# The start of a two-layer hybrid decoder: order of the first loads, and of ScalarE's first work

## The chip, the cores and the metric

The kernel runs on one core of a Trainium2 chip, in one launch. The metric is the device time of an execution in microseconds (us); lower is better. The engines are TensorE (PE in the profile; PEld are its weight loads), VectorE (DVE), ScalarE (ACT), GpSimd (POOL) and SyncE (SP), which only issues DMAs. ScalarE and GpSimd issue DMAs too.

## The reference

Two layers over 512 tokens of width 1024, in float32. Each layer normalizes x, projects it once, feeds four mixers (short convolution, sparse attention, gated recurrence, cross-attention into 256 memory tokens), sums them through gates, and ends with a SwiGLU feed-forward block. What matters here is the memory's path, which is computed before the layers, and the first norm of x:

```python
mem_n = rmsnorm(mem, mem_norm)
...
h = rmsnorm(x, norm_mix)                          # per layer; x @ w_in follows
...
mk, mv = jnp.split(mem_n @ mem_w_kv, 2, axis=-1)  # per layer, 1024 x 1024 weights
mk = rmsnorm(mk.reshape(b, MEM_TOKENS, MEM_HEADS, MEM_HEAD_DIM), mem_k_norm)
```

## The kernel before

**Products.** A float32 operand is written as a high and a low part in float32r, and a product is three matmuls (`mm3`, lines 260 to 262): high by high, high by low, low by high. So weights must be split before TensorE can use them. Class `Chunk` loads 1 MB of weights into a buffer `w_raw` (two of them, DMA issued by SyncE), and splits it in two parts of 128x1024: ScalarE copies to `w_hi` (line 97, through the helper `A`), and VectorE subtracts to `w_lo` (line 225). There are three buffers of each part.

**The order of the work.** The program is written as a list of operations. A compile-time scheduler sets the order on each engine from the order of the program, a priority (`tc.high_priority(offset=AHEAD)` puts the splits far ahead) and a simulated timeline. On the chip each engine and each DMA-issuing queue works through its list in order, so an operation that waits holds up all behind it on its engine. `tc.add_manual_dep(..., order, ...)` adds an order without a semaphore: it only says what comes first in that list.

**The start**, in the order of the program:

1. Constants, masks and 14 warm-up matmuls (`WARM`, line 144).
2. The memory is loaded whole into `mem_in` (line 150). Eight small loads bring the norms' gains and other parameters as 78 rows into the tile `rows` (line 157): those below row 40 from ScalarE's queue, the others from SyncE's. One transpose (line 160) turns them into columns, which ScalarE copies to `prm`. From there come the gains `g_mem`, `g_mix` and so on.
3. GpSimd's queue loads the four gains of the sparse attention's norms (lines 182 and 188, `gq_raw`, `gk`) and the positions (line 314); VectorE scales two of them (line 185).
4. `mem_in_T` transposes the memory, 8 columns of tiles by 2 (line 376). Each transposed column goes through one of the three `tr` buffers in PSUM; ScalarE writes `mt_hi`, multiplied by the gain, VectorE `mt_lo` (line 378). Then ScalarE squares and sums the memory for its norm (`mem_sq`).
5. `steps(mem_kv(0), first_h())` runs two generators in turn. `mem_kv` takes four chunks of the weights `mem_w_kv` of its layer, two for the keys and two for the values; each is 48 matmuls of 256 columns (8 tiles of the inner dimension, 2 of tokens, 3 by `mm3`). `first_h` loads x in two halves (line 391), squares it for its norm, transposes it (line 410) and writes the two parts of `h` (line 273), two columns of tiles at a step.
6. `rope_tables()` is VectorE's work. `mem_kv(1)` does the memory's keys and values for the second layer. Then the layers begin; their first product reads `h`.

Of the kernel before, what the change touches and what calls it, by code (L numbers as in the profile page):

```python
# [21 lines left out]
P = 128  # L22
S = 512
NT = S // P
D = 1024
# [44 lines left out]
def hybrid_trunk(ctx: ExitStack, tc: tile.TileContext, x, mem, positions, norm_mix, w_in, conv_w,  # L70
# [75 lines left out]
    n_rows = 78  # L146
# [3 lines left out]
    nc.sync.dma_start(mem_in, mem[0].rearrange("(t p) d -> p t d", p=P))  # L150
    for lo, src in ((0, norm_mix.rearrange("l (c p) -> (l c) p", p=P)),
                    (16, norm_ffn.rearrange("l (c p) -> (l c) p", p=P)),
                    (32, mem_norm.rearrange("(c p) -> c p", p=P)),
                    (40, conv_w.rearrange("l w (c p) -> (l w c) p", p=P)),
                    (64, hgrn_lower_bounds.rearrange("l (c p) -> (l c) p", p=P)),
                    (72, hgrn_out_norm), (74, mem_q_norm), (76, mem_k_norm)):
        (nc.scalar if lo < 40 else nc.sync).dma_start(rows[lo:lo + src.shape[0], :], src)
    prm = consts.tile([P, n_rows], F32, name="prm")
    ps = tr_ps()
    pe.transpose(ps[:, :n_rows], rows[:n_rows, :], ident[:n_rows, :n_rows])  # L160
    A(prm, ps[:, :n_rows], AF.Copy)
# [7 lines left out]
    def g_mem(c):  # L169
        return prm[:, 32 + c:33 + c]  # L170

    def g_conv(l, w, c):
        i = 40 + (l * 3 + w) * 4 + c
# [37 lines left out]

    class Chunk:
        def __init__(self, src, kt, n):
            self.kt, self.step = kt, min(kt, 1024 // n)
            raw = wpool.tile([P, 2048], F32, name="w_raw", bufs=RAW_BUFS)[:, :kt * n].rearrange("p (k n) -> p k n", n=n)
            nc.sync.dma_start(raw, src.rearrange("(k p) n -> p k n", p=P))
            self.parts = []
            for k in range(0, kt, self.step):
# [4 lines left out]
                with tc.high_priority(offset=AHEAD):  # L223
                    A(hi, raw[:, k:e], AF.Copy)
# [17 lines left out]
    def features(w, a, js, k0=0, kt=None, pss=None):  # L242
        """Feature-major products of the 128-column tiles js of a chunk."""
# [127 lines left out]

    def mem_in_T():
        for c in range(KD):
# [3 lines left out]
            A(mt[0][:, c, :], ps[:, :MEM], AF.Copy, scale=g_mem(c))  # L377
            dve.scalar_tensor_tensor(mt[1][:, c, :], ps[:, :MEM], g_mem(c), f(mt[0][:, c, :]),
                                     op0=OP.mult, op1=OP.subtract)
        for t in range(2):  # L380
            A(mem_sq, mem_in[:, t, :], AF.Square, scale=D ** -0.5, accum_out=mem_ss[:, t:t + 1])
# [6 lines left out]
    def first_h():  # L388
        xin = sp.tile([P, NT, D], F32, name="xin")
        for hf in range(2):  # L390
            nc.sync.dma_start(xin[:, 2 * hf:2 * hf + 2, :],
                              x[0, hf * 2 * P:(hf + 1) * 2 * P, :].rearrange("(t p) d -> p t d", p=P))
# [3 lines left out]
        for t in range(NT):  # L396
            A(mem_sq, xin[:, t, :], AF.Square, scale=D ** -0.5, accum_out=xs[:, t:t + 1])
# [19 lines left out]
    def mem_kv(l):  # L417
# [687 lines left out]
```

## Time and profile before

| | |
|---|---|
| timed runs | 2059.12 us median of 3 (2059.05 to 2059.2) |
| span of the profiled execution | 2057.1 us, 27077 instructions |
| timed runs less that span | 1.9 to 2.1 us, outside the first and last instruction |
| TensorE busy | 2046.8 us (99%) |
| VectorE, ScalarE, GpSimd busy | 1270.5, 1017.1, 9.8 us |
| granted TensorE clock, mean | 0.999 |
| DMA | 203.83 MB, mean 99 GB/s |

The span is that of one execution taken by the hardware profiler, from the first to the last instruction. The profile gives no time of that execution beside the span; the timed runs are other executions.

How to read its lines: a timeline has the start in us, the duration, engine, line of the kernel, operation, what is written `<-` what is read, shapes, and in brackets how long the engine had been idle and what ended that. A group's line has busy time, mean duration in ns and the idle time before it with its releaser. The chain of waits follows the work that ended last back through whatever released it. Matmuls overlap, so their durations are longer than the distance from one to the next.

### The profile page before, as it was taken

The page shows a single profiled execution, that of the slowest core. Times are in us where ns is not written, and L with a number is a line of the kernel's source. Part 1 is how long each engine was busy: PE and PEld are TensorE (multiplying, and loading weights), DVE is VectorE, ACT ScalarE, POOL GpSimd, SP SyncE. Part 2 cuts the span into 40 slices and gives each one's busy share as a digit, 9 for nine tenths or more (in the row PEclk, how much of TensorE's full clock was granted, in tenths as well). Part 3 has the DMA queues.
Part 4 walks back from the last instruction along what each step waited for, and adds up shares of the span by engine and source line. Part 5 has one row for each costly group of instructions (what it writes and reads, how often), then busy time and mean ns, then how long its engine had stood idle before and what let it go on. Part 6 is the DMA issues. An engine that isn't in the chain of part 4 may idle for free.

```text
span 2057.1 us, 27077 instructions
## 1 busy us (share of the span) xinstructions
PE 2046.8 (99%) x10588; PEld 1731.1 (84%) x10588; DVE 1270.5 (62%) x2513; ACT 1017.1 (49%) x1836; POOL 9.8 (0%) x33
## 2 busy tenths in 40 slices
PE   8999999999999999999999999999999999999999
PEld 8998988888888888888889898888888888888889
DVE  6779998547676544334457899953766754532542
ACT  7654655856665423223355456576657643322321
POOL 0000000000000000000000000000000000000000
PEclk9999999999999999999999999999999999999999
DMA  7632222212233232232242223321223332322322
GB/s 255 215 95 86 72 89 93 81 53 92 82 113 113 83 102 92 92 114 92 87 154 93 88 75 97 97 66 62 83 82 109 116 102 83 103 93 92 103 72 93
DMA packets 190783, 203.83 MB, mean 99 GB/s; under 512 B 4270, under 2 KB 182528, under 8 KB 190528
## 3 DMA queue, kind: packets, MB, share of 16 engines
q1 hardware_dynamic: 186944, 193.56, 29.2%
q10 hardware_dynamic: 3552, 8.41, 1.1%
q8 instruction: 83, 1.36, 0.3%
q14 instruction: 44, 0.36, 0.1%
q0 software_dynamic: 160, 0.13, 0.0%
HBM read 191.60 MB, written 10.49 MB: 98 GB/s over the span
## 4 chain that ended last, share of the span: by engine, by line
PE 98%; DMA 1%; DVE 0%; ACT 0%; SPq 0%; issue 0%; DVEq 0%; ACTq 0%
PE mm L261 30%; PE mm L260 30%; PE mm L262 30%; PE tr L705 1%; PE tr L699 1%; PE at L676 1%; PE at L675 1%; PE at L927 1%; DMA w_raw<-in_mem_w_kv_dram 1%; PE at L928 0%; PE at L260 0%; PE at L262 0%; PE at L261 0%; PE at L952 0%; PE tr L643 0%; PE tr L744 0%
## 5 line engine op out<-in xcount | busy, mean ns | idle before, releaser
L261 PE MATMUL mm<-h_lo,w_hi 128*128 128x512 f32 x1664 | 652.1, 392 | 0.0
L260 PE MATMUL mm<-h_hi,w_hi 128*128 128x512 f32 x1664 | 651.8, 392 | 0.0
L262 PE MATMUL mm<-h_hi,w_lo 128*128 128x512 f32 x1664 | 649.5, 391 | 0.0
L225 DVE TENSOR_TENSOR w_lo<-w_raw,w_hi 128x1024 fp32r<-128x1024 f32 (+1 forms) x348 | 419.7, 1207 | 350.7 <-ACT w_hi L97 349.5
L97 ACT ACTIVATE w_hi<-w_raw 128x1024 fp32r<-128x1024 f32 (+1 forms) x348 | 363.5, 1046 | 469.6 <-PE mm L261 416.8
L261 PEld LDWEIGHTS mm<-h_lo,w_hi 128*128 128x128 f32 x1664 | 312.6, 188 | 64.9 <-issue 2.5
L262 PEld LDWEIGHTS mm<-h_hi,w_lo 128*128 128x128 f32 x1664 | 312.4, 188 | 65.1 <-issue 1.4
L260 PEld LDWEIGHTS mm<-h_hi,w_hi 128*128 128x128 f32 x1664 | 312.6, 188 | 64.5 <-issue 2.0
L262 PE MATMUL mm<-w_hi,h_lo 128*128 128x256 f32 (+1 forms) x448 | 128.0, 286 | 0.0
L261 PE MATMUL mm<-w_lo,h_hi 128*128 128x256 f32 (+1 forms) x448 | 126.8, 284 | 0.0
L260 PE MATMUL mm<-w_hi,h_hi 128*128 128x256 f32 (+1 forms) x448 | 126.8, 285 | 0.0
L261 PE MATMUL mm<-a_lo,w_hi 128*128 128x512 f32 x272 | 106.1, 390 | 0.0
L260 PE MATMUL mm<-a_hi,w_hi 128*128 128x512 f32 x272 | 105.9, 389 | 0.0
L262 PE MATMUL mm<-a_hi,w_lo 128*128 128x512 f32 x272 | 105.6, 390 | 0.0
L260 PE MATMUL mm<-y_hi,w_hi 128*128 128x512 f32 x256 | 101.3, 397 | 0.0
L262 PE MATMUL mm<-y_hi,w_lo 128*128 128x512 f32 x256 | 100.2, 392 | 0.0
L261 PE MATMUL mm<-y_lo,w_hi 128*128 128x512 f32 x256 | 100.1, 391 | 0.0
L262 PEld LDWEIGHTS mm<-w_hi,h_lo 128*128 128x128 f32 x448 | 85.6, 191 | 1.4 <-issue 0.8
L260 PEld LDWEIGHTS mm<-w_hi,h_hi 128*128 128x128 f32 x448 | 85.2, 191 | 1.2 <-issue 0.8
L261 PEld LDWEIGHTS mm<-w_lo,h_hi 128*128 128x128 f32 x448 | 85.5, 191 | 0.6
L97 ACT ACTIVATE a_hi<-fg 128x512 fp32r<-128x512 f32 x44 | 27.8, 633 | 109.0 <-DVE fg L1054 109.0
L97 ACT ACTIVATE prob<-prob,small 128x128 f32<-128x128 f32 (+3 forms) x128 | 69.2, 555 | 15.2 <-DVE small L688 14.6
(351 smaller groups left out, 3048.6 us busy)
## 6 DMA issues: line engine op xcount, KB each, us to landing
w_raw<-in_w_in_dram SPq DMA_DIRECT2D x72, 1024.0 KB, 5.0
w_raw<-in_ffn_w_up_dram SPq DMA_DIRECT2D x44, 1024.0 KB, 5.1
w_raw<-in_w_lift_dram SPq DMA_DIRECT2D x32, 512.0 KB, 3.4
w_raw<-in_ffn_w_down_dram SPq DMA_DIRECT2D x16, 1024.0 KB, 5.0
w_raw<-in_mem_w_kv_dram SPq DMA_DIRECT2D x8, 1024.0 KB, 5.2
w_raw<-in_w_out_dram SPq DMA_DIRECT2D x8, 1024.0 KB, 4.9
kv<-kv ACTq DMA_DIRECT2D x8, 512.0 KB, 7.4
xT<-x_spill SPq DMA_DIRECT2D x16, 256.0 KB, 5.8
```

Of the source, the lines that this page charges most:

```text
L97: i = act.activation(dst, src, func, **kw)
L225: dve.tensor_sub(lo, raw[:, k:e], f(hi))
L260: pe.matmul(ps, ah, bh, start=first, stop=False)
L261: pe.matmul(ps, ah, bl, start=False, stop=False)
L262: pe.matmul(ps, al, bh, start=False, stop=last)
L675: pe.matmul(ps, q[:, hh, s], k[0][:, :n], start=True, stop=False)
L676: pe.matmul(ps, q[:, hh, s], k[1][:, :n], start=False, stop=True)
L699: pe.transpose(pp[:, (2 * e + i) * P:(2 * e + i + 1) * P], probs[2 * i + e][:, b * P:(b + 1) * P], ident)
L705: pe.matmul(pv[e * HD:(e + 1) * HD, :], vt[:, b, :], pt[:, b, e * 2 * P:(e + 1) * 2 * P], start=b == 0, stop=b == t)
L927: pe.matmul(pa[:, s], z[:, s], cmr[:, s], start=True, stop=True)
```

## The change

- The memory's gain is no longer among the 70 `rows` but is loaded as a tile of its own, `mem_row`, first on SyncE's queue, and transposed and copied to `mem_g` by itself. The transpose of `rows` and the copy to `prm` come after the memory's transposes in the program.
- The memory and the first weight chunk (`raw0`) are loaded in halves in turn: memory columns 0 to 511, weight rows 0 to 511, then the others. `Chunk` takes `raw0` instead of loading it.
- The small loads: convolution weights and recurrence bounds move from SyncE's queue to ScalarE's, the last three rows to GpSimd's.
- ScalarE's order: a chunk of layer 0's keys has its splits behind the memory copies that it needs (first part behind copy 4, second behind copy 8; the second chunk behind the last copy). The memory's squares come behind the last copy. x's squares come behind the last split that exists when `first_h` reaches them.
- `first_h` yields twice before it starts, so that the third chunk has been issued, and x's loads come behind it on SyncE's queue.

The diff without the renumbered rows and columns and a removed docstring:

```diff
@@ -143,22 +143,33 @@
     for _ in range(WARM):
         pe.matmul(ps[:, :P], ones_d, ones_d, start=True, stop=True)
     rows = sp.tile([P, P], F32, name="rows")
-    n_rows = 78
+    n_rows = 70
     warm = consts.tile([P, 1], F32, name="warm")
     A(warm, one, AF.Exp)
     mem_in = sp.tile([P, 2, D], F32, name="mem_in")
-    nc.sync.dma_start(mem_in, mem[0].rearrange("(t p) d -> p t d", p=P))
+    mem_row = sp.tile([KD, P], F32, name="mem_row")
+    nc.sync.dma_start(mem_row, mem_norm.rearrange("(c p) -> c p", p=P))
+
+    def w_raw(kt, n):
+        return wpool.tile([P, 2048], F32, name="w_raw", bufs=RAW_BUFS)[:, :kt * n].rearrange("p (k n) -> p k n", n=n)
+
+    raw0 = w_raw(KD, 256)
+    for hf in range(2):
+        cs = slice(hf * D // 2, (hf + 1) * D // 2)
+        nc.sync.dma_start(mem_in[:, :, cs], mem[0][:, cs].rearrange("(t p) d -> p t d", p=P))
+        nc.sync.dma_start(raw0[:, hf * KD // 2:(hf + 1) * KD // 2],
+                          mem_w_kv[0][cs, 0:256].rearrange("(k p) n -> p k n", p=P))
     for lo, src in ((0, norm_mix.rearrange("l (c p) -> (l c) p", p=P)),
                     (16, norm_ffn.rearrange("l (c p) -> (l c) p", p=P)),
-                    (32, mem_norm.rearrange("(c p) -> c p", p=P)),
-                    (40, conv_w.rearrange("l w (c p) -> (l w c) p", p=P)),
-                    (64, hgrn_lower_bounds.rearrange("l (c p) -> (l c) p", p=P)),
-                    (72, hgrn_out_norm), (74, mem_q_norm), (76, mem_k_norm)):
-        (nc.scalar if lo < 40 else nc.sync).dma_start(rows[lo:lo + src.shape[0], :], src)
+                    (32, conv_w.rearrange("l w (c p) -> (l w c) p", p=P)),
+                    (56, hgrn_lower_bounds.rearrange("l (c p) -> (l c) p", p=P)),
+                    (64, hgrn_out_norm), (66, mem_q_norm), (68, mem_k_norm)):
+        (nc.scalar if lo < 64 else nc.gpsimd).dma_start(rows[lo:lo + src.shape[0], :], src)
+    mem_g = sp.tile([P, KD], F32, name="mem_g")
+    ps = tr_ps()
+    pe.transpose(ps[:, :KD], mem_row, ident[:KD, :KD])
+    A(mem_g, ps[:, :KD], AF.Copy)
     prm = consts.tile([P, n_rows], F32, name="prm")
-    ps = tr_ps()
-    pe.transpose(ps[:, :n_rows], rows[:n_rows, :], ident[:n_rows, :n_rows])
-    A(prm, ps[:, :n_rows], AF.Copy)
 
     def g_mix(l, c):
         return prm[:, l * KD + c:l * KD + c + 1]
@@ -167,10 +178,10 @@
         return prm[:, 16 + l * KD + c:16 + l * KD + c + 1]
 
     def g_mem(c):
-        return prm[:, 32 + c:33 + c]
+        return mem_g[:, c:c + 1]
 
     def g_conv(l, w, c):
-        i = 40 + (l * 3 + w) * 4 + c
+        i = 32 + (l * 3 + w) * 4 + c
         return prm[:, i:i + 1]
 
     def col(i):
@@ -209,11 +220,14 @@
         dve.scalar_tensor_tensor(e, z, 0.0, e, op0=OP.min, op1=OP.subtract)
         A(dst, e, AF.Exp)
 
+    loads, splits = [], []
+
     class Chunk:
-        def __init__(self, src, kt, n):
+        def __init__(self, src, kt, n, raw=None, after=None):
             self.kt, self.step = kt, min(kt, 1024 // n)
-            raw = wpool.tile([P, 2048], F32, name="w_raw", bufs=RAW_BUFS)[:, :kt * n].rearrange("p (k n) -> p k n", n=n)
-            nc.sync.dma_start(raw, src.rearrange("(k p) n -> p k n", p=P))
+            if raw is None:
+                raw = w_raw(kt, n)
+                loads.append(nc.sync.dma_start(raw, src.rearrange("(k p) n -> p k n", p=P)))
             self.parts = []
             for k in range(0, kt, self.step):
                 e = min(kt, k + self.step)
@@ -221,7 +235,10 @@
                 hi, lo = (wpool.tile([P, 1024], F32R, name=nm, bufs=W_BUFS)[:, :m].rearrange("p (k n) -> p k n", n=n)
                           for nm in ("w_hi", "w_lo"))
                 with tc.high_priority(offset=AHEAD):
-                    A(hi, raw[:, k:e], AF.Copy)
+                    split = A(hi, raw[:, k:e], AF.Copy)
+                    splits.append(split)
+                    if after is not None:
+                        tc.add_manual_dep(split.ins, after[e - 1].ins.name, order, reason="after the copies")
                     dve.tensor_sub(lo, raw[:, k:e], f(hi))
                 self.parts.append((range(k, e), hi, lo))
 
...
@@ -369,16 +386,19 @@
     mt = (sp.tile([P, KD, MEM], F32R, name="mt_hi"), sp.tile([P, KD, MEM], F32R, name="mt_lo"))
     mem_r2, mem_r4 = small(4, name="mem_r2", bufs=1), small(4, name="mem_r4", bufs=1)
 
+    copies = []
+
     def mem_in_T():
         for c in range(KD):
             ps = tr_ps()
             for t in range(2):
                 pe.transpose(ps[:, t * P:(t + 1) * P], mem_in[:, t, c * P:(c + 1) * P], ident)
-            A(mt[0][:, c, :], ps[:, :MEM], AF.Copy, scale=g_mem(c))
+            copies.append(A(mt[0][:, c, :], ps[:, :MEM], AF.Copy, scale=g_mem(c)))
             dve.scalar_tensor_tensor(mt[1][:, c, :], ps[:, :MEM], g_mem(c), f(mt[0][:, c, :]),
                                      op0=OP.mult, op1=OP.subtract)
         for t in range(2):
-            A(mem_sq, mem_in[:, t, :], AF.Square, scale=D ** -0.5, accum_out=mem_ss[:, t:t + 1])
+            square = A(mem_sq, mem_in[:, t, :], AF.Square, scale=D ** -0.5, accum_out=mem_ss[:, t:t + 1])
+            tc.add_manual_dep(square.ins, copies[-1].ins.name, order, reason="after the copies")
         rstd_into(mem_r, mem_ss, small, 2)
         dve.tensor_copy(mem_r4.rearrange("p (a b) -> p a b", b=2), mem_r[:, :, None].to_broadcast([P, 2, 2]))
         dve.tensor_mul(mem_r2, mem_r4, mem_r4)
@@ -386,15 +406,20 @@
     norms = []
 
     def first_h():
+        yield
+        yield
         xin = sp.tile([P, NT, D], F32, name="xin")
+        last_load, last_split = loads[-1], splits[-1]
         for hf in range(2):
-            nc.sync.dma_start(xin[:, 2 * hf:2 * hf + 2, :],
-                              x[0, hf * 2 * P:(hf + 1) * 2 * P, :].rearrange("(t p) d -> p t d", p=P))
+            i = nc.sync.dma_start(xin[:, 2 * hf:2 * hf + 2, :],
+                                  x[0, hf * 2 * P:(hf + 1) * 2 * P, :].rearrange("(t p) d -> p t d", p=P))
+            tc.add_manual_dep(i.ins, last_load.ins.name, order, reason="after the weights")
         xs = small(NT, "xs", 1)
         r_t = small(NT, "rstd_t", 2)
         r_b = state.tile([P, S], F32, name="rstd", bufs=1)
         for t in range(NT):
-            A(mem_sq, xin[:, t, :], AF.Square, scale=D ** -0.5, accum_out=xs[:, t:t + 1])
+            square = A(mem_sq, xin[:, t, :], AF.Square, scale=D ** -0.5, accum_out=xs[:, t:t + 1])
+            tc.add_manual_dep(square.ins, last_split.ins.name, order, reason="after the weights")
         rstd_into(r_t, xs, small, NT)
         ps = tr_ps()
         for t in range(NT):
@@ -414,10 +439,11 @@
                 yield
         nc.scalar.dma_start(x_dram, xc)
 
-    def mem_kv(l):
+    def mem_kv(l, raw=None):
         kv = sp.tile([P, 4, 2, 2, MEM], F32R, name="kv", bufs=1)
         for q in range(2):
-            w = wchunk(mem_w_kv[l][:, q * 256:(q + 1) * 256], KD, 256)
+            w = Chunk(mem_w_kv[l][:, q * 256:(q + 1) * 256], KD, 256, raw if q == 0 else None,
+                      (copies if q == 0 else copies[-1:] * KD) if l == 0 else None)
             kus = []
             ms, r = small(4), small(4, "mk_r", 2)
             for t in range(2):
...
@@ -457,7 +483,10 @@
             nc.scalar.dma_start(kv_dram[l][:, 2 * q:2 * q + 2, 1], f(kv[:, 2 * q:2 * q + 2, 1]))
             yield
     mem_in_T()
-    steps(mem_kv(0), first_h())
+    ps = tr_ps()
+    pe.transpose(ps[:, :n_rows], rows[:n_rows, :], ident[:n_rows, :n_rows])
+    A(prm, ps[:, :n_rows], AF.Copy)
+    steps(mem_kv(0, raw0), first_h())
     rope_tables()
     steps(mem_kv(1))
     start.close()
...
```

More of the change, by code (lines that the diff above doesn't have):

```diff
@@ L443, in mem_kv @@
                 hi, lo = kv[:, 2 * q + j, 0, 0, :], kv[:, 2 * q + j, 0, 1, :]
-                A(hi, ps, AF.Copy, scale=col(76 + l))
-                dve.scalar_tensor_tensor(lo, ps, col(76 + l), f(hi), op0=OP.mult, op1=OP.subtract)
+                A(hi, ps, AF.Copy, scale=col(68 + l))
+                dve.scalar_tensor_tensor(lo, ps, col(68 + l), f(hi), op0=OP.mult, op1=OP.subtract)
             nc.scalar.dma_start(kv_dram[l][:, 2 * q:2 * q + 2, 0], f(kv[:, 2 * q:2 * q + 2, 0]))
@@ L468, in hybrid_trunk @@
     inv = consts.tile([P, H4], F32, name="inv")
-    a0, a1 = prm[:, 64:68], prm[:, 68:72]
+    a0, a1 = prm[:, 56:60], prm[:, 60:64]
     mx, e0, e1, sm, z0 = (small(H4, name=f"lb{i}", bufs=1) for i in range(5))
@@ L604, in mem_branch @@
                     with tc.high_priority(offset=AHEAD):
-                        A(qh, pq, AF.Copy, scale=col(74 + l))
+                        A(qh, pq, AF.Copy, scale=col(66 + l))
                         A(sq, pq, AF.Square)
-                        dve.scalar_tensor_tensor(ql, pq, col(74 + l), f(qh), op0=OP.mult, op1=OP.subtract)
+                        dve.scalar_tensor_tensor(ql, pq, col(66 + l), f(qh), op0=OP.mult, op1=OP.subtract)
                     pm = tr_ps()
```

2 lines of the change are left out of this document (1 added, 1 removed).

## The prediction

> **What bounds the kernel now.** I read the page first, then the chain of waits of the first 22 us, then the timelines of the engines there. From the page:
>
> ```profile
> span 2057.1 us, 27077 instructions
> PE 98%; DMA 1%; DVE 0%; ACT 0%; SPq 0%; issue 0%; DVEq 0%; ACTq 0%
> ```
>
> TensorE is the bound for 98% of the span. The edit touches only the start, so it can win only what TensorE loses before its stream of products becomes gapless. Three rows of TensorE's timeline show where that is:
>
> ```profile
> 1.12 5.04 PE L144 MATMUL tr<-ones_d 128*128 128x128 f32 x28 [1.12 <-DVE ones_d L118]
> 8.09 0.26 PE L160 MATMUL tr<-ident,rows 78*128 78x78 f32 x1 [1.94 <-DMA rows<-in_mem_k_norm_dram]
> ...
> 22.03 0.39 PE L261 MATMUL mm<-w_lo,mt_hi 128*128 128x256 f32 x1 [0.54 <-DVE w_lo L225]
> 22.25 0.28 PE L262 MATMUL mm<-w_hi,mt_lo 128*128 128x256 f32 x1
> 22.37 0.28 PE L260 MATMUL mm<-w_hi,mt_hi 128*128 128x256 f32 x1
> ```
>
> The warm-up ends at 6.16, the transpose of the parameter rows waits for a DMA until 8.09, and from 22.03 one 256-column product follows another every 0.12 us. The next window holds 46.47 busy us of 46.60, so nothing is lost behind 22.03:
>
> ```profile
> 22.00:68.60 46.60, 46.47 (x388) 46.12 (x389) 36.64 (x109) 36.13 (x91) 0.52 (x1) 1.00 0.75 255
> ```
>
> (TensorE, weight loads, VectorE, ScalarE and GpSimd busy, clock, DMA share, GB/s.) What TensorE did from 6 to 22 us, by groups:
>
> ```profile
> L260 PE MATMUL mm<-w_hi,mt_hi 128*128 128x256 f32 x17 | 5.4, 328 | 0.8 <-ACT w_hi L97 0.8
> L261 PE MATMUL mm<-w_lo,mt_hi 128*128 128x256 f32 x16 | 5.2, 333 | 0.8 <-DVE w_lo L225 0.8
> L262 PE MATMUL mm<-w_hi,mt_lo 128*128 128x256 f32 x16 | 5.2, 335 | 0.0
> L376 PE MATMUL tr<-ident,mem_in 128*128 128x128 f32 x16 | 3.1, 290 | 0.9 <-DVE mt_lo L378 0.9
> ```
>
> That is 49 products (the first chunk's 48 and one of the second) and 16 transposes. At 0.12 us each, with a transpose counted as a product (it has half the columns, so this is high), they need 65 x 0.12 = 7.8 us. They ended at 22.03, 15.9 us after the warm-up. Some 8.1 us is therefore all that can be won. The chain of waits says what took it:
>
> ```profile
> 0.81 5.40 DMA mem_in<-in_mem_dram
> 6.22 0.23 SPq L157
> ...
> 6.95 0.58 SPq L391
> ...
> 8.08 11.56 DMA w_raw<-in_mem_w_kv_dram
> 19.66 1.07 ACT w_hi L97
> 20.75 1.24 DVE w_lo L225
> ```
>
> The second weight chunk is issued behind x (L391), lands at 19.64, is split on ScalarE and VectorE, and only then TensorE runs free. The first chunk is issued after the wait of the sixth row load:
>
> ```profile
> SPq L157 <- DMA mem_in<-in_mem_dram: 3.5, 1, 3.5
> ```
>
> That load (6.22) is the ninth transfer of the SP and ScalarE queues together and waits for the first, the memory; that the ninth waits for the first is my reading.
>
> **The change, part by part.** Loads first. SP issues mem_row, half of the memory, half of chunk 0, the other halves, then chunk 1; x comes behind chunk 2.
>
> ```profile
> w_raw<-in_mem_w_kv_dram SPq DMA_DIRECT2D x8, 1024.0 KB, 5.2
> rows<-in_norm_mix_dram ACTq DMA_DIRECT2D x1, 8.0 KB, 3.2
> DMA packets 1539, 3.11 MB, mean 388 GB/s; under 512 B 42, under 2 KB 1027, under 8 KB 1539
> ```
>
> The last row is the window 8 to 16, with loads queued behind each other: 388 GB/s. The whole memory landed at 6.21; half of it is 0.52 MB less, 1.35 us, and its issue comes some 0.3 us later behind mem_row (0.23 for such an issue in the chain): 5.2. Each further half adds 1.35: chunk 0's first half 6.5, memory's second 7.9, chunk 0's second 9.2, and chunk 1 (2.7) at 11.9 instead of 19.64. The ninth transfer still waits for the first, but that is now a row of 4 KB (by the 8 KB row, 3.2 after issue, about 4.0), while the queue has bytes to move until 9. This costs nothing; if it hung on the first memory half (5.2) it still would not.
>
> One rule speaks against the halves. The Trainium skill, page "DMA: Bandwidth & Descriptors", section Bandwidth, advises batches of 1 MiB or more; by its fixed 2.0 us and 436 GB/s an isolated half would take 3.2 us, an estimate. The 388 GB/s of loads in a queue speaks for overlap; what a serial cost would do is rival 4.
>
> Now the engines. Their distances in the trace, from the rows' transpose at 8.09 on:
>
> ```profile
> 8.47 0.22 ACT L97 ACTIVATE prm<-tr 128x78 f32<-128x78 f32 x1
> 8.80 0.82 ACT L97 ACTIVATE mt_hi<-tr,prm 128x256 fp32r<-128x256 f32 x2
> 9.29 1.40 DVE L378 SCALAR_TENSOR_TENSOR mt_lo<-tr,prm,mt_hi 128x256 fp32r<-128x256 f32 x3
> 9.82 1.35 PE L376 MATMUL tr<-ident,mem_in 128*128 128x128 f32 x6 [0.65 <-DVE mt_lo L378]
> 11.51 2.00 ACT L97 ACTIVATE w_hi<-w_raw 128x1024 fp32r<-128x1024 f32 x2 [0.70 <-DMA w_raw<-in_mem_w_kv_dram]
> 12.59 1.23 DVE L225 TENSOR_TENSOR w_lo<-w_raw,w_hi 128x1024 fp32r<-128x1024 f32 x1 [0.85 <-ACT w_hi L97]
> 13.87 0.39 PE L261 MATMUL mm<-w_lo,mt_hi 128*128 128x256 f32 x1 [0.76 <-DVE w_lo L225]
> ```
>
> - The gain's transpose now needs mem_row alone (landed by 4) and starts when the warm-up ends: 6.17 instead of 8.09. Its copy (0.22) takes the place of prm's; the 70 rows' transpose goes behind the memory's work, where TensorE waits anyway.
> - First mt_hi 0.71 later, 6.88; first mt_lo 1.20 later, 7.37, done at 7.84 (0.47 each). The fourth column's transpose waits for that buffer (8.09 to 9.82 is 1.73): 7.90; its mt_hi about 0.5 later (less than the 0.71, which holds the gain's copy too), 8.4 to 8.8.
> - The order edge puts the first split behind that copy: w_hi 8.8 to 9.85 (its data landed at 6.5), w_lo 1.08 behind its start, 9.9 to 11.1, and the first full product 1.28 behind that: 11.2 instead of 13.87.
> - Second half: mt_lo of column 5 waits for w_lo, 11.1 to 11.6; the last column's transpose needs that buffer, its copy ends about 12.3. Second w_hi 12.3 to 13.3, w_lo 13.4 to 14.6, its products from 14.7. The first half's 24 products end at 11.2 + 2.9 = 14.1; the second half's 24 start at 14.7 and end at 17.6.
> - Chunk 1 (landed 11.9) is split on ScalarE 13.3 to 15.3 and on VectorE to 17.0; its first part is ready at 15.9, ahead of 17.6.
>
> So the gapless stream begins at 17.5 or so where it began at 22.03: 4.5 us won. The squares of the memory (two of 1.06 us that stood ahead of everything on ScalarE) move behind the copies; the norm they feed is first used behind chunk 0, and ScalarE has room there. Chunk 2 needs chunk 0's buffer (14.6) and 5.2 us to land, 19.8, split by 22.2; TensorE wants it at 17.5 + 48 x 0.12 = 23.3. Chunk 3 queues behind x: 19.8 + 8.1 (three chunks' bytes at 388 GB/s) is 27.9, split by 30.3, wanted at 29.1 and later by the key transposes. That is tight, about 1 us either way, and x's 32 transposes can fill it.
>
> The three small rows go to GpSimd's queue. Ahead of what?
>
> ```profile
> 1.34 0.71 POOL L182 DMA_DIRECT2D gq_raw<-in_dsa_q_norm_dram  x1 [0.34 <-issue]
> ...
> 2.92 0.57 POOL L182 DMA_DIRECT2D gq_raw<-in_dsa_q_norm_dram  x1
> ...
> 6.82 0.19 DVE L185 TENSOR_SCALAR gq<-gq_raw 128x64 f32<-128x64 f32 x1 [5.17 <-DMA gq_raw<-in_dsa_q_norm_dram]
> 7.52 0.20 DVE L185 TENSOR_SCALAR gq<-gq_raw 128x64 f32<-128x64 f32 x1 [0.50 <-DMA gq_raw<-in_dsa_q_norm_dram]
> ```
>
> Three issues of 0.57 to 0.71 us push both gq loads (and positions, and the masks' selects) back by 1.7 to 2.1 us. The gq multiplies wait for them on VectorE, and whatever the compiler queued behind them waits too: rival 1. Two more row loads on ScalarE's queue delay only the warm-up activation, which nobody waits for.
>
> Sum: the profiled span is 2057.1 and the timed runs lie at 2059.05 to 2059.2, so 2.0 us lie outside it and stay. Span 2052.6, time 2059.1 - 4.5 = **2054.6**. A measurement can tell about 0.2% from no change, here 4.1 us, so the forecast is just beyond it. If TensorE gets hi-hi products during its waits, more comes, up to the 8.1 bound: 2051.0.
>
> **Rivals.**
>
> 1. VectorE stands behind the gq loads. They now land at 8.5 and 9.2 to 9.6, and my first mt_lo is at 7.37. If both stand ahead of it, it starts at 9.5, everything slides by 2.0, and 2.5 are won: 2056.6. For it: both were ahead of every mt_lo before (6.82 and 7.52 against 9.29). Against: the compiler's order goes by readiness, and mt_lo is earlier now.
>
> 2. The clock drops again. For these three us it stood at 0.50:
>
> ```profile
> 15.00:18.00 3.00, 3.00 (x16) 3.00 (x16) 2.19 (x12) 2.97 (x7) 0.00 (x0) 0.50 1.06 366
> ```
>
> Half of 3 us is 1.5 lost: 3.0 won, 2056.1. Before, part of that loss lay under the wait for chunk 1; now nothing would hide it. Against: by 14.8 TensorE would have done some 24 products, where it had done 11 (2 and then one every 0.12 us from 13.87). The Trainium skill, page "TensorE: Matmul & The Clock Gate", Part 1, says that about 3.4 us without work halve the clock and 3.4 us of work restore it; by that rule the edit's shorter waits would keep it whole, and the trace agrees that sparse work preceded the drop.
>
> 3. ScalarE becomes the bound, and it is slower. From 22.0 to 68.6 it worked 36.1 of 46.6 us, 78%. x's squares move behind the third chunk's splits:
>
> ```profile
> 14.49 1.06 ACT L97 ACTIVATE mem_sq<-xin 128x1024 f32<-128x1024 f32 x1
> ...
> 15.67 1.06 ACT L97 ACTIVATE mem_sq<-xin 128x1024 f32<-128x1024 f32 x1
> ...
> 57.69 0.74 DVE L273 SCALAR_TENSOR_TENSOR h_lo<-xc,prm,h_hi 128x512 fp32r<-128x512 f32 x1
> ...
> 68.67 0.40 PE L260 MATMUL mm<-h_hi,w_hi 128*128 128x512 f32 x1
> ```
>
> From one square to the next it is 1.18. That puts 4 x 1.18 = 4.7 us of squares, and 2.4 of the memory's, into that stretch: 43.2 us. At 78% it takes 55.4 us from 17.5, so h's first product comes at 72.9 instead of 68.67: 4.2 us slower, 2063.3. It decides once ScalarE cannot be used above 43.2 / (64.2 - 17.5) = 93%. Against: much of its idle time was waiting for TensorE, which now comes earlier, and h had 10 us to spare.
>
> 4. The halves pay their fixed part in series, so the edit does not do what it says: 5.2 less 2.7 for the bytes is 2.5 us per load, two loads more are 5.0, and the 4.5 are gone: 2059.1.
>
> **How the numbers follow.** The forecast, 2054.6, has 0.42, more than the 4.5 won through hi-hi products 0.12; rival 1 has 0.18, rival 2 0.11, rival 4 0.03, rival 3 0.14. The first two are faster by over 0.2%: 0.54. Rivals 1, 2 and 4 lie within 0.2%: 0.32. Rival 3 is slower: 0.14. The range goes from 2051.0 (the bound) to 2058.1 (rivals 1 and 2 together win 1.0); rivals 3 and 4 are left out.
>
> **What would show it.** Right: the gain's transpose at 6.2, first full product near 11, chunk 1 landed near 12, no gap behind 17.5, h's first product near 64, and the same distance from there to the end. The waits name what failed: mt_lo late behind gq (rival 1), the clock at 0.50 (2), TensorE waiting for h or for mm's copies (3), halves landing 4 us apart (4). The forecast is wrong if the distance from h's first product to the end changes by more than 1 us, since the compiler reorders everything behind the start too and I costed that at nothing.

## The result

| | us |
|---|---|
| before, median of 4 | 2059.16 (2059.05 to 2059.71) |
| after, median of 4 | 2070.81 (2069.48 to 2073.45) |
| ratio | 1.0057, 95% interval 1.0043 to 1.0071 |

The kernel is 11.65 us slower; 2054.6 was forecast, and the range ended at 2058.1. The profiled execution is the longest of the four, 2073.45 us with a span of 2071.6; their 4 us of spread go with the granted clock (0.997 to 0.999).

**The profile after.** TensorE's timeline of the start (start, duration, engine, line, operation; in brackets the idle time before it and what ended it), followed by two rows of ScalarE's:

```profile
6.04 0.22 PE L170 MATMUL tr<-ident,mem_row 8*128 8x8 f32 x1
...
11.40 0.58 PE L278 MATMUL mm<-w_lo,mt_hi 128*128 128x256 f32 x1 [1.18 <-DVE w_lo L242]
...
15.48 0.38 PE L395 MATMUL tr<-ident,mem_in 128*128 128x128 f32 x2
15.62 0.37 PE L279 MATMUL mm<-w_hi,mt_lo 128*128 128x256 f32 x1
15.82 0.23 PE L487 MATMUL tr<-ident,rows 70*128 70x70 f32 x1
17.37 0.50 PE L277 MATMUL mm<-w_hi,mt_hi 128*128 128x256 f32 x2 [1.32 <-ACT w_hi L97]
18.32 0.58 PE L277 MATMUL mm<-w_hi,mt_hi 128*128 128x256 f32 x1 [0.44 <-ACT w_hi L97]
```

```profile
15.90 0.47 ACT L97 ACTIVATE mt_hi<-tr,mem_g 128x256 fp32r<-128x256 f32 x1 [5.13 <-PE tr L395]
16.27 1.99 ACT L97 ACTIVATE w_hi<-w_raw 128x1024 fp32r<-128x1024 f32 x2
```

The gain's transpose and the first full product come when forecast (6.2 and 11.2). But the last two of the memory's 16 transposes (15.48) stand behind 23 of the first half's 24 products in TensorE's list. ScalarE idles 5.13 us for them, and its fixed order holds the second split and chunk 1's behind that copy. Chunk 2's buffer is late with them, as SyncE's queue shows (the first row spans chunks 1 and 2, so chunk 2 is issued at 18.6; then x):

```profile
3.33 15.64 SPq L230 DMA_DIRECT2D w_raw<-in_mem_w_kv_dram  x2
19.02 2.41 SPq L414 DMA_DIRECT2D xin<-in_x_dram  x2
```

The windows (TensorE, weight loads, VectorE, ScalarE, GpSimd busy, clock, DMA share, GB/s) show the clock at half for most of two of them, DMA standing still in one, and the clock low again at 90:

```profile
11.00:15.00 4.00, 3.60 (x18) 3.60 (x19) 2.08 (x8) 0.00 (x0) 0.00 (x0) 0.57 0.73 240
15.00:18.00 3.00, 1.55 (x12) 1.16 (x10) 1.13 (x2) 2.10 (x3) 0.00 (x0) 1.00 0.00 0
18.00:22.00 4.00, 3.68 (x18) 3.66 (x19) 3.17 (x7) 4.00 (x11) 0.00 (x0) 0.57 0.55 184
86.00:90.00 4.00, 2.73 (x24) 2.65 (x23) 2.51 (x4) 1.32 (x4) 0.00 (x0) 0.98 0.99 313
90.00:97.00 7.00, 7.00 (x36) 7.00 (x35) 1.81 (x10) 2.47 (x11) 0.66 (x3) 0.52 0.12 46
```

Two later rows of TensorE's timeline, h's first product (68.67 before) and the first layer's attention into the memory, whose keys come back from memory by a load that stands behind the fourth load of `w_in` on SyncE's queue (the row in the second fence):

```profile
72.47 0.39 PE L277 MATMUL mm<-h_hi,w_hi 128*128 128x512 f32 x1
88.93 0.39 PE L277 MATMUL at<-mk,qg_hi 128*128 128x256 f32 x1 [1.26 <-DMA mk<-kv]
```

```profile
82.68 0.88 SPq L626 DMA_DIRECT2D mk<-kv  x2
```

That load was issued at 77.22 before, and nothing waited for it.

Where the time went can be read by matching the n-th matmul behind the warm-up in both traces: after is 0.3 us late at the 100th (some 26 us), 3.7 at the 450th (68 us), 8.0 at the 600th (91 us), 9.0 at the 3000th, and 15.2 near the end. The last 7 us come in two stretches far from the edit, one in each layer, where TensorE waits no longer than before (0.09 us in all behind 100 us, in both kernels). The groups of the page show them, before above, after below (busy us, mean ns of one):

```profile
L260 PE MATMUL mm<-y_hi,w_hi 128*128 128x512 f32 x256 | 101.3, 397 | 0.0
L260 PE MATMUL mm<-mg_hi,w_hi 128*128 128x512 f32 x128 | 49.3, 389 | 0.0
L260 PE MATMUL mm<-a_hi,w_hi 128*128 128x512 f32 x272 | 105.9, 389 | 0.0
```

```profile
L277 PE MATMUL mm<-y_hi,w_hi 128*128 128x512 f32 x256 | 102.6, 402 | 0.0
L277 PE MATMUL mm<-mg_hi,w_hi 128*128 128x512 f32 x128 | 50.1, 395 | 0.0
L277 PE MATMUL mm<-a_hi,w_hi 128*128 128x512 f32 x272 | 105.9, 389 | 0.0
```

The products of `y` (mixer outputs) and `mg` (merged) take 5 to 6 ns more each, those of `a` and `h` do not. With the low parts there are 768 and 384 of them; their mean distance from one start to the next (those over 0.3 us apart left out) goes from 0.2277 to 0.2335 us, and 1152 x 0.0058 = 6.7 us.

### The profile page after: what moved, and what is told of

It reads as the page before. It is cut to its first block, busy times and chain, and to the rows that moved or that the text cites. A ratio compares the mean times of both kernels' runs of the same rounds, so it can differ in the third digit from the quotient of the medians.

```text
span 2071.6 us, 27094 instructions
## 1 busy us (share of the span) xinstructions
PE 2058.8 (99%) x10589; PEld 1735.5 (84%) x10589; DVE 1271.6 (61%) x2513; ACT 1017.5 (49%) x1837; POOL 11.3 (1%) x36
## 4 chain that ended last, share of the span: by engine, by line
PE 96%; DMA 2%; ACT 1%; DVE 1%; issue 0%; POOL 0%; ACTq 0%; SPq 0%; POOLq 0%; DVEq 0%
PE mm L278 29%; PE mm L279 29%; PE mm L277 29%; PE tr L734 1%; PE tr L728 1%; PE at L705 1%; PE at L704 1%; DMA w_raw<-in_mem_w_kv_dram 1%; PE at L956 1%; ACT w_hi L97 1%; DMA w_raw<-in_w_in_dram 0%; DVE w_lo L242 0%; PE at L957 0%; PE at L277 0%; PE at L279 0%; PE at L278 0%
## 5 line engine op out<-in xcount | busy, mean ns | idle before, releaser
L97 ACT ACTIVATE prob<-prob,small 128x128 f32<-128x128 f32 (+3 forms) x128 | 69.2, 554 | 15.3 <-DVE small L717 14.7
```

The source lines that it names most:

```text
L97: i = act.activation(dst, src, func, **kw)
```

## The experiments

Three things changed together: the addresses, the start, and the stretch from 67 to 92 us. "Late" below is the lag behind the kernel before at the 450th and at the 600th matmul, in the profiled execution.

### Addresses

`prm` shrank from 78 columns to 70. By the addresses in the compiled programs, the later tiles of its side of the on-chip memory that live through the layers (h, the split weights, a) moved down by 32 B; y and mg are allotted from the other end and stayed. In the kernel before, the first `w_hi` buffer lay at byte 79968 of a partition and the first `y_hi` at 186208: 106240 apart, 415 times 256 B. Padding `prm` back to 78 columns gives the kernel that is called aligned from here on.

```diff
-    warm = consts.tile([P, 1], F32, name="warm")
+    warm = consts.tile([P, 9], F32, name="warm")[:, :1]      # before, 32 B; 17, 33, 65 for 64, 128, 256 B
-    prm = consts.tile([P, n_rows], F32, name="prm")
+    prm = consts.tile([P, 78], F32, name="prm")[:, :n_rows]  # after, aligned
```

> The kernel before, with one constant made 32 B longer, so that the tiles behind it (h, a, the split weights) lie 32 B further while y and mg, which are allocated from the other side, stay. Nothing else differs. Theory of the addresses (a product is slower where its moving operand and its weights do not lie alike in 64 B): the products of y and mg go from 0.227 to 0.234 us apart, 1152 of them, and the time from 2059.2 to about 2066.5 us (2065.0 to 2068.0). Rival (the late 7 us of the kernel after come from its other order, or from the clock): 2059.2, within 1 us, and y and mg stay at 0.227.

> The kernel after, with prm allocated 78 columns wide instead of 70, so that every later tile lies where it did in the kernel before. Theory of the addresses: y and mg go back to 0.227 us per product and the time from 2070.8 to about 2063.5 us (2062 to 2066, some of it the clock); what is left over 2059.2 is the start's. Rival (order or clock): 2070.8, within 2 us, y and mg at 0.234.

> The kernel before, with the same constant made 64 B longer instead of 32 B. Theory of the addresses in its narrow form (what counts is how the moving operand and the weights lie to each other within 64 B): y and mg stay at 0.227 us per product and the time at 2059.2, within 1 us. Rival (any move of the weights against y and mg costs, or the longer constant itself does): as with 32 B, y and mg at 0.234 and about 2066.

> The kernel before with the weights, h and a moved by 128 B against y and mg. Whether the place within 128 B counts: then y and mg stay at 0.227 us per product and the time at about 2059. Rival (the place within 256 B or more, or any move): 0.234 and about 2066.

> The same with 256 B. Whether the place within 256 B counts: then y and mg stay at 0.227 us and the time at about 2059 (the distance of y's tile to the split weights before is a multiple of 256 B, not of 512). Rival (any move costs): 0.234 and about 2066.

| kernel | y less weights, mod 256 B | y's product, mean ns | us |
|---|---|---|---|
| before | 0 | 397 | 2059.1 to 2059.4 |
| after | 32 | 402 | 2070.81 |
| before, weights up 32 B | 224 | 402 | 2066.17 |
| before, 64 B | 192 | 401 | 2066.11 |
| before, 128 B | 128 | 401 | 2065.32 (one execution) |
| before, 256 B | 0 | 397 | 2059.62 (one execution) |
| after, aligned | 0 | 397 | 2063.96 |

The 32 B alone cost the kernel before 6.9 us (ratio 1.0034, 1.0021 to 1.0046), and taking them back saves the kernel after 6.85. The narrow theory of 64 B fell: 64 and 128 B cost as much as 32, and 256 B cost nothing. The groups of the kernel with 32 B and of that with 256 B:

```profile
L260 PE MATMUL mm<-y_hi,w_hi 128*128 128x512 f32 x256 | 102.6, 402 | 0.0
```

```profile
L260 PE MATMUL mm<-y_hi,w_hi 128*128 128x512 f32 x256 | 101.3, 397 | 0.0
```

h and a lie a multiple of 256 B from the weights in every one of these kernels, and never slow down. Last, y and mg were moved instead, by a 32 B tile behind them in the kernel after:

```diff
+                pads.append(mix.tile([P, 8], F32, name="pad"))
+                dve.memset(pads[0], 0.0)
```

> The kernel after as it is (prm 70 columns), with y and mg moved by the same 32 B as the weights, by a small tile behind them in their own pool (one short memset per layer). Theory (what counts is where y and mg lie to the weights within 256 B, not where either lies): y and mg at 0.227 us per product and 2062 to 2066 us, as the aligned kernel. Rival (the weights' or h's own place counts): 0.234 and 2070 to 2072.

Its group of the same products:

```profile
L277 PE MATMUL mm<-y_hi,w_hi 128*128 128x512 f32 x256 | 101.2, 397 | 0.0
```

The pace came back, so it is the distance that counts and not either place. The time, 2067.24, came down by 3.6 only and missed the 2062 to 2066 expected: behind the 600th matmul this kernel loses nothing, but there it was already 10.4 us late (after: 8.0), with the same wait for mk, 1.80 us here, and another of 2.89 behind it.

### The last transposes

```diff
-                tokens(w, mt, t, ps)
+                tokens(w, mt, t, ps, after=trs[-1] if l == 0 and q == 0 else None)   # first product behind the last transpose
```

> The aligned kernel, and chunk 0's first product kept behind the last transpose of the memory on TensorE. Theory of the fixed order (ScalarE's last copy of the memory waited 5.1 us for two transposes that the compiler had put behind 22 products, and the second split and chunk 1's stood behind it): that wait falls under 1 us, the second split starts at about 12.5 us instead of 16.3, chunk 2 is issued at about 15 instead of 18.6, h's first product comes at about 69 instead of 72.5, and the time is 3 to 4 us under the aligned kernel, 2059.5 to 2060.5. Rival (x comes too late and ScalarE is the bound of 45 to 70 us whatever the start does): h's first product stays at 71.5 to 72.5 and the time within 1 us of the aligned kernel.

Measured: 2058.9 us, 5.1 under the aligned kernel (medians of ten; these executions spread from 2056.4 to 2062.8, the aligned kernel's from 2061.4 to 2069.1). ScalarE's timeline, where the kernel after has the two rows shown above:

```profile
12.93 0.47 ACT L97 ACTIVATE mt_hi<-tr,mem_g 128x256 fp32r<-128x256 f32 x1 [1.09 <-PE tr L397]
13.30 1.05 ACT L97 ACTIVATE w_hi<-w_raw 128x1024 fp32r<-128x1024 f32 x1
```

Against the kernel after, the wait of 5.13 became 1.09, and the second split comes 3.0 us earlier. h's first product is at 67.56 (aligned: 72.56). The wait for mk is gone as well: late by -1.2 and -1.4 us, where the aligned kernel has 3.8 and 5.5. Against the kernel before, the ratio is 0.9999 (0.9989 to 1.0008): the loss is mended, and a gain is not told from none.

The other way to free the second split is to drop ScalarE's fixed order (the edges of the splits and of the memory's squares):

```diff
-                    if after is not None:
-                        tc.add_manual_dep(split.ins, after[e - 1].ins.name, order, reason="after the copies")
...
-            tc.add_manual_dep(square.ins, copies[-1].ins.name, order, reason="after the copies")
```

> The aligned kernel without the fixed order on ScalarE (no edges from the memory's copies to the splits and to the memory's squares); halves, gain tile and late x stay. Theory (ScalarE stands idle for 5.1 us only because the order holds the splits behind the last copy): the second split and chunk 1's no longer wait for the last copy, ScalarE's idle time ahead of 16 us falls under 2 us, chunk 2 is issued before 17, and the time is 2 to 5 us under the aligned kernel, 2059 to 2062. Rival (the transposes behind the products are the fault, whatever ScalarE's order): the second half's products still wait for the last copy at 15.9, within 1 us of the aligned kernel, 2063 to 2065.

Measured: 2065.52 us, not better than the aligned kernel and outside both expectations. The start itself gains (chunk 2 is issued at 14.7, and the 100th matmul comes 1.1 us ahead of before), but then a wait comes on TensorE at 34.84, and the clock is low from 36.1 to 39.5 (TensorE's timeline):

```profile
34.84 0.39 PE L275 MATMUL mm<-w_hi,mt_hi 128*128 128x256 f32 x1 [2.21 <-DVE kv L479]
```

A wait of 2.64 us follows at 88.17. Without the edges the compiler orders other work differently too, and which of these waits comes from the missing order was not separated. What is shown is that with the order kept, fixing TensorE's list pays, and that dropping the order does not.

### The halves

In the kernel with the transposes first, the memory and chunk 0 are loaded whole, one after the other.

```diff
-    for hf in range(2):
-        cs = slice(hf * D // 2, (hf + 1) * D // 2)
+    for hf in range(1):
+        cs = slice(0, D)
```

> The aligned kernel with the transposes first (2058.9 us), the memory and chunk 0 loaded whole, one after the other, instead of in halves. Theory of the prediction (the halves let the first transposes and the first split begin before all has landed): the first transposes of the memory, chunk 0's first product and chunk 2's load come 1 to 2 us later, and the time is 1 to 2 us more, 2060 to 2061. Rival (the halves bring nothing, since the last column, not the first, sets the first product): within 0.7 us of 2058.9.

The first split in ScalarE's timeline:

```profile
12.46 1.06 ACT L97 ACTIVATE w_hi<-w_raw 128x1024 fp32r<-128x1024 f32 x1 [2.42 <-DMA w_raw<-in_mem_w_kv_dram]
```

ScalarE waits 2.42 us for the whole chunk, the first split starts at 12.46 instead of 9.70, and the 100th matmul comes 2.4 us later than with halves. The time is 2062.91, 4.0 more where 1 to 2 were expected; the rest of it is a wait for mk again (1.61 us at 87.36) and the low clock behind it (87.5 to 90.9). So the halves are worth having. But the memory's first transposes come no later with whole loads (6.72, with halves 7.27; both right behind the warm-up): the gain shown is that of the half chunk, and one by the half memory is not seen.

### Where x is loaded

Five runs moved x's loads; the lines below stand for the place of the edit in all of them.

```diff
     def first_h():
-        yield
-        yield          # x early: neither, and no edges on x; x behind two chunks: one of them
```

> The aligned kernel with x's two loads back where they were in the kernel before (without the two empty steps and the edges on x's loads and squares). Theory of late x (x's squares and splits, moved into ScalarE's full stretch of 45 to 70 us, cost the time): h's first product comes 2 to 4 us earlier than in the aligned kernel, 68.5 to 70.5, and the time is 2060 to 2061.5. Rival (fixed order at the start): chunk 1 lands later behind x, the start is no better, h's first product at 72 to 73, and the time within 1 us of the aligned kernel or up to 2 us more.

> The aligned kernel with both edits: chunk 0's first product behind the last transpose of the memory, and x's loads where they were before the change. Theory of two separate causes (the transposes gave 5.1 us, the early x 2.8): the gains add up in part, h's first product comes at 65.5 to 67.5, 2056 to 2058 us. Rival (one cause: both edits only spare the wait of layer 0's attention for mk and what stands behind it): no more than the transposes alone gave, 2058.5 to 2059.5.

> The kernel before with only x put behind three weight chunks (two empty steps, and the edges on x's loads and squares). Theory (late x puts x's squares and splits into ScalarE's full stretch, about 2.8 us by the run with x early): 2060.5 to 2062.5, h's first product at 70 to 72. Rival (late x is worth having by itself, since chunk 1 lands sooner, and only hurts behind the blocked start): 2057 to 2059.5, h's first product at 68.7 or earlier.

> The aligned kernel with chunk 0's first product behind the transposes, and x behind two chunks (0 and 1) instead of three: one empty step instead of two, the same edges. Theory (x belongs in the queue's idle time between chunk 1, which the start needs by about 18 us, and chunk 2, whose buffer comes free at 15: in front of chunk 1 it starves the start, behind chunk 2 it delays chunk 3 and all that follows): no wait of TensorE over 0.6 us between 13 and 66 us, h's first product at 65.5 to 67, 2055.5 to 2057.5 us. Rival (the place of x is worth nothing more once the start runs without a stall): 2058 to 2060, as with x behind three chunks.

> The kernel before with only x put behind chunks 0 and 1 (where three chunks cost 10 us). Theory: chunk 2 and chunk 3 come when they came before, so that the 10 us are gone; 2057 to 2060, h's first product at 67.5 to 69. Rival (any later x costs, through x's squares and splits on ScalarE): 2062 to 2068.

| kernel | x behind | late, 450th | 600th | mk's load issued | us |
|---|---|---|---|---|---|
| before | chunk 0 | 0 | 0 | 77.22 | 2059.1 to 2059.4 |
| before | 3 chunks | 2.5 | 9.7 | 84.17 | 2069.42 |
| before | 2 chunks | 1.3 | 7.6 | 82.98 | 2066.01 |
| aligned | 3 chunks | 3.8 | 5.5 | 83.01 | 2063.96 |
| aligned | chunk 0 | 0.9 | 3.9 | 84.36 | 2061.17 |
| transposes first | 3 chunks | -1.2 | -1.4 | 75.95 | 2058.90 |
| transposes first | 2 chunks | -0.95 | 5.3 | 81.52 | 2064.55 |
| transposes first | chunk 0 | 1.9 | 1.8 | 79.53 | 2060.85 |

The first expectation held (h's first product at 69.65); the theories of the other four fell, and of their rivals only the last one's range was met. x behind three chunks costs the kernel before 10.3 us by itself, more than three times the 2.8 expected, and most of it between the 450th and the 600th matmul. x behind two chunks, which was to cure that, costs 6.8 there. With the transposes first, x early is 2 us worse: chunk 1 then comes behind x, TensorE waits for its split, and the clock is low from 23.1 to 26.5 (TensorE's timeline):

```profile
21.52 0.50 PE L277 MATMUL mm<-w_hi,mt_hi 128*128 128x256 f32 x2 [1.66 <-ACT w_hi L97]
```

And x behind two chunks, the fastest start of all (2.6 us ahead of before at the 100th matmul), throws away 6.2 us behind the 450th. So the place of x decides less by the start than by what happens at 67 to 92 us.

### From 67 to 92 us

The chain of waits of the kernel with the transposes first and x behind two chunks has these two pieces (start, duration):

```profile
61.44 12.89 DMA w_raw<-in_w_in_dram
...
81.52 6.31 DMA mk<-kv
```

The second load of `w_in` took 12.89 us, where the same load took 9.4 in the kernel before (issued at 61.78). The store of x to memory, 2 MB in one DMA, was issued at 61.6, beside it; in the kernel before at 55.1. The fourth load of `w_in` waits for the second's buffer, and mk stands behind the fourth. To test this, the store was put later in the kernel before, and cut into eight of 256 KB from GpSimd's queue, each as soon as its column of x is copied, in three kernels:

```diff
-        nc.scalar.dma_start(x_dram, xc)
+            nc.gpsimd.dma_start(x_dram[:, c, :], xc[:, c, :])    # cut: in the loop over c
+            if l == 1 and q == 0:
+                nc.scalar.dma_start(x_dram, xcs[0])              # or later: behind the first values of mem_kv(1)
```

> The kernel before with x's store to memory (2 MB, issued at 55.1 us) put behind the second layer's first store of memory values (63.3 us); nothing else moved. Theory of the collision (in every slow kernel this store is issued at 61.7 to 64.5, a load of layer 0's weights then takes 9.4 to 12.9 us instead of 5.2, and mk's load stands behind it on SyncE's queue): one load of w_in takes over 9 us, TensorE waits over 1 us between 80 and 92, and the time is 2062 to 2067. Rival (the store is harmless and late mk comes from x's late arithmetic): 2059.2, within 1 us.

> The kernel with the transposes first and x behind two chunks (2064.6 us, w_in load of 12.9 us), its store of x cut into eight of 256 KB, each issued by GpSimd as its column of x is copied. Theory of the collision: no load of w_in over 8 us, TensorE's wait for mk goes, and the time falls by 4 to 7 us, 2057.5 to 2060.5. Rival: within 1 us of 2064.6.

> The kernel with the transposes first and x behind three chunks (2058.9 us; store of x at 59.1, no wait for mk), with the same cut store. Theory: the collision was avoided there already, so at most 1 us better, 2057.5 to 2059.5. Rival (the cut store itself, on GpSimd's queue, costs or gains by itself): outside of that.

> The kernel before with only the cut store. Theory: nothing to gain, since the store is issued at 55.1 ahead of the loads of w_in; 2058.5 to 2060. Rival (the store delays something there too): 2056 to 2058.

With the cut store the kernel with x behind two chunks goes from 2064.55 to 2058.77 us, late by 0.6 and 0.4. ScalarE's row of that split shows when the load (issued at 63.00) was there:

```profile
71.03 1.06 ACT L97 ACTIVATE w_hi<-w_raw 128x1024 fp32r<-128x1024 f32 x1 [1.82 <-DMA w_raw<-in_w_in_dram]
```

That is 8.0 us instead of 12.89; mk is issued at 78.14, and no wait for it is left. (The cut store also changed the compiler's order: the 100th matmul comes 1.7 us later than without the cut.) Two more traces show the slow load. In the kernel before with x behind three chunks it was issued at 64.33, 0.2 us ahead of the store, and ScalarE's split waited for it until 12.8 us later:

```profile
77.18 1.06 ACT L97 ACTIVATE w_hi<-w_raw 128x1024 fp32r<-128x1024 f32 x1 [6.20 <-DMA w_raw<-in_w_in_dram]
```

With x behind two chunks there, it was issued at 63.04, again 0.2 us ahead of the store, and the split waited until 76.00.

The three other results bound the theory. The late store by itself does nothing to the kernel before in the median (2059.41), against the expectation: in the profiled execution it was issued at 63.7, 1.9 us behind the load, and no wait came of it, though four of the ten executions took 2061.5 to 2064.8. In that execution the load's split begins at 68.86 without a wait, and at 68.68 in the kernel before with the cut store, at most 7.1 us behind its issue in both; in the kernel before itself it waits until 71.20. So the early store seems to slow this load there too (the 5.2 us of the expectation are those of other loads), and TensorE did not have to wait for it. Where there was no wait for mk, the medians with the cut store are 1.5 us (2057.42) and 0.9 us lower (2058.13, the kernel before, between the two ranges expected); with executions that spread over 1 to 6 us, neither is told from no change. The first of these is the fastest kernel here: against the kernel before the ratio is 0.9993 (0.9984 to 1.0002).

What is shown, then: in three kernels a store issued 0.2 us behind this load goes with 12.8 to 13.0 us for it; cutting the store cures this stretch in the one slow kernel where it was tried; and a store that is late by itself does not bring it about. In the kernel after itself the store (64.5) was 3.3 us ahead of the load, which took 9.42, no longer than before, but was issued 6.0 us later; there the wait for mk follows from the late start, and went with it. The cut store was not tried there.

## Why the prediction was wrong

**The step that failed first** is the one that put the last column's transpose behind column 5's `mt_lo`, at 11.6. It stood behind 23 products, at 15.48. The prediction followed what each operation waits for, and not the order in which TensorE's list would hold them, which the compiler sets. The trace of the kernel before had shown it: there the last two transposes stood behind 27 products, and it cost little, since ScalarE had done both splits of chunk 0 by then (TensorE's timeline):

```profile
18.47 0.39 PE L376 MATMUL tr<-ident,mem_in 128*128 128x128 f32 x2
```

The edges on ScalarE made that order costly: everything from the second split on was pinned behind a copy whose input TensorE was free to postpone. Undoing it gave 5.1 us. From it follow the second split (16.27 for 12.3), chunk 2's issue (18.6 for 14.6) and 5 of the 8.5 us by which h's first product is late (72.47, where about 64 was forecast; 67.56 with the transposes first).

**The term left out** was the largest. The prediction costed everything behind h's first product at nothing and named a change there of over 1 us as what would make it wrong. That distance went from 1988.4 to 1999.1 us in the profiled executions. 6.9 us of it are the addresses, by the eight columns of `prm` that no step looked at. The rest, 3.8 us, goes with the wait for mk (1.26 us) and the low clock behind it (6.8 us at half speed); in the profiled execution of the aligned kernel, with a wait of 1.73 us there and no such drop, the distance is 0.8 us longer than before.

**What held.** The gain's transpose (6.04 for 6.17), the first `mt_lo` (7.24 for 7.37), the first full product (11.40 for 11.2) and a gain by the halves. The loads landed near the forecast up to the second half of the memory (8.4 for 7.9), but chunk 1 only at 15.1, where 11.9 was forecast; with the transposes first its split begins at 15.29 for 13.3. With the two faults mended (aligned, transposes first) TensorE runs from 12.46 to 32.69 without a wait, and its 100th matmul comes 2.1 us earlier than before. That is half of the 4.5. About 1.7 (half of 3.4 us, an estimate) went to the clock, which was at half from 13.6 to 17.0; before, the prediction noted, part of that loss lay under the wait for chunk 1. Another 0.8 us is lost by the 200th matmul, with the wait at 32.69 for a split, where the prediction had called chunk 3 tight.

**The rivals.** Rival 1 came true by 0.4 us, on `w_lo` and not on `mt_lo`: `w_lo` stood behind the gq load until 10.13, while its `w_hi` was done at 9.67. Rival 4 is refuted by the run with whole loads; in the kernel after the halves landed 1.3 to 2.6 us apart. Rival 3 named the right sign and h's first product within half a microsecond (72.9), but not the mechanism: with the transposes first, the same squares in the same place leave it at 67.56, so ScalarE was not the bound. Rival 2 happened and was underpriced. In the kernel after, the clock was at half from 11.3 to 14.7, from 18.2 to 21.6 and from 89.8 to 96.6, which is 13.7 us at half speed against 3.4 before. How much of it falls into the start goes with the execution: the kernel before and the four with moved addresses have the same start, and 0 to 6.8 us at half speed in it, with the 100th matmul within 0.3 us in all five, so there it was hidden. The Trainium skill, page "TensorE: Matmul & The Clock Gate", Part 1, puts a drop behind a window of about 3.4 us without work; the prediction concluded from it that shorter waits would keep the clock whole. The trace does not agree: the first drop came in a wait of 1.18 us, the last behind one of 1.26, at the end of four us in which TensorE was busy for 2.73.

## What to carry to other kernels

When an edit changes the size of a constant, look at where everything behind it lands: a kernel bound by TensorE can lose or win 0.3% by the distance between its operands alone, and a run with only the padding changed tells. A fixed order on one engine is only as good as the order on the engine that feeds it; fix both or neither. A transfer that moves changes what it meets, and the bill may come where a later load queues behind it, tens of microseconds on, so compare the traces product by product and not at the place of the edit alone.

## What the hardware showed beyond the expected

- In this kernel, products of 128x512 float32r start 0.227 us apart when the moving operand lies a multiple of 256 B from the weight buffers, and 0.232 to 0.234 us apart (medians) at 32, 128, 192 or 224 B more. The Trainium skill, page "SBUF — State Buffer", section "SBUF: two separate sides", says that on the engines' side only the port shared by VectorE and GpSimd causes contention and that TensorE never waits for another; these runs show that TensorE's own accesses are not free of addresses. What in the chip does it was not tried.
- From 18 us on, each drop of the clock before the end of the program (the kernel after and nine experiments) began within 2.5 us behind a wait of TensorE of 1.0 to 2.2 us, but waits of 1.73 (aligned) and 2.64 us (without the fixed order) were followed by none. The length of the wait is thus not enough to tell. In each trace all changes of the clock lie whole multiples of 3.41 us apart, and in the 3.41 us ahead of each of the 31 drops, the early ones included, TensorE was busy for 25 to 69% by the profile. No stretch of this grid at full clock with over 70% was followed by a drop; some with less were not either (47% in the run without the fixed order), so what decides is still open. In the kernel after, the first, second and fifth of these windows (columns as above) ended in a drop, the third and fourth, with waits of 0.88 and 1.19 us, did not:

```profile
7.91:11.32 3.41, 1.86 (x10) 0.98 (x10) 2.38 (x6) 2.54 (x6) 0.00 (x0) 1.00 0.82 221
14.73:18.15 3.42, 1.82 (x14) 1.43 (x12) 1.28 (x2) 2.25 (x3) 0.00 (x0) 1.00 0.00 0
35.21:38.62 3.41, 2.53 (x19) 2.34 (x20) 3.01 (x5) 3.41 (x10) 0.00 (x0) 1.00 0.44 164
65.93:69.34 3.41, 2.64 (x22) 2.67 (x23) 3.41 (x10) 3.41 (x9) 0.00 (x0) 1.00 1.08 432
86.41:89.83 3.42, 2.15 (x19) 2.07 (x19) 2.10 (x4) 0.92 (x3) 0.00 (x0) 1.00 0.99 314
```

- A load of 1 MB that was issued 0.2 us ahead of a store of 2 MB on another queue took 12.8 to 13.0 us in three kernels. It took 8.0 when the store was cut into eight, and at most 7.1 when the store came 1.9 us behind it.
